# Four tap-row transfers replaced by one ScalarE copy, with a new table of priorities, in a four-layer encoder on one core

## The chip, the cores and the metric

One Trainium2 chip, of which the program uses a single core. The metric is device time in microseconds (us): the median of the runs, 1069.27 us before the change. The core's engines are TensorE (PE in the profile; PEld is its weight load), VectorE (DVE), ScalarE (ACT) and GpSimd (POOL); SyncE (SP) sends transfers, and its queue is SPq. The granted clock is the share of its full rate at which TensorE is allowed to run.

## The reference

The kernel computes a stack of four residual layers over x of 1 x 512 x 1024 in float32: differential attention, a Conformer convolution module, latent attention (MLA), and differential attention again. Every layer has one input projection, which also emits a SiLU gate, and one output projection. The change is in the second layer:

```python
def _conformer_conv(h, w_in, b_in, conv_w, conv_b, ln_g, ln_b, w_out):
    proj = h @ w_in + b_in
    a, b, gate = jnp.split(proj, 3, axis=-1)
    u = a * jax.nn.sigmoid(b)
    u = lax.conv_general_dilated(
        u, conv_w[:, None, :].astype(u.dtype), window_strides=(1,),
        padding=[(B_CONV - 1, 0)], dimension_numbers=('NWC', 'WIO', 'NWC'),
        feature_group_count=B_WIDTH) + conv_b
    u = jax.nn.silu(_layer_norm(u, ln_g, ln_b))
    return (u * jax.nn.silu(gate)) @ w_out
```

The convolution is depthwise: each of the 1024 channels has 31 taps of its own along the 512 positions. `b_conv_w` holds the taps, 31 rows by 1024 channels.

## The kernel before

Every fp32 product is made of three TensorE matmuls: both operands are split into a rounded high part and a low part, and hi·hi, lo·hi and hi·lo are added. In the profile these are the pairs on `Hh` and the single ones on `Hl`; such three matmuls of 512 columns are called a group below. A weight is loaded by SyncE (`..._w_r`), cast to its high part on ScalarE, and its low part is made by a subtraction on VectorE or GpSimd. The layers are named L0 to L3 in the program; the profile leaves the number away, so `L_qk_a` is the query and key projection's accumulator of some layer.

**The start of L0.** x is transposed on TensorE, 128 positions by four channel blocks at a time (`L0_tr00` to `L0_tr34`: the first digit is the block of positions, the second the first channel block). ScalarE copies a transpose into X and squares X, channel block by channel block in ascending order (`L0_sqs`, then `L0_sq1` to `sq7`); GpSimd adds the seven others to the first (line 521), and TensorE sums over the channels with `L0_ss`. The first square needs the blocks 0 to 3 of all positions, so nothing of this sum begins before `tr00`, `tr10`, `tr20` and `tr30` are done.

**The end of L0.** The last heads' attention, the gate's last chunk (`L0_g1`) and the first half of the output projection (`L0_o0`) are mixed. `L_ytr` transposes the gated heads, ScalarE makes the high part `L_y` of them (line 494), VectorE the low part (line 530), and `L_o` multiplies them with the output weights. The moves of `L_qk_st` (line 568) shift queries and keys between partitions for the last heads. In this place the tables of the second layer are prepared too: `L_rows` (taps and biases of `b_conv_w`, `b_conv_b`, `b_b_in`) is loaded and transposed to `L_vtr`.

**The convolution of L1.** Its eight channel blocks of 128 are handled by three engines, by the string 'DPDPDYYY': blocks 0, 2 and 4 on VectorE (a multiply and add per tap), blocks 1 and 3 on ScalarE and GpSimd (`L_ct`, `L_cq`), blocks 5, 6 and 7 on TensorE (`conv_phase`). For TensorE the input u is laid out in shifted phases by 48 moves on SyncE (`L_u<-L_u`, line 568; 16 for each block), and four taps at a time are multiplied as 32 x 32 diagonal matrices. The taps for those matrices come from `wx`, which `phase_weights` fills: `rows4` holds, for each of 12 sets of 32 channels, the 31 taps four times side by side; twelve TensorE transposes (`L_wxt`) turn it, and four ScalarE copies shift it into `wx`. `rows4` was loaded by four transfers from `b_conv_w` (line 562), each 31 x 12 x 32 elements, 46.5 KB in runs of 128 bytes. The profile shows both tiles, `L1_rows` and `L1_rows4`, as `L_rows`.

**What sets the order.** The program is written as a list of nodes in a `Plan` (class at line 362): each node has an engine, an assumed cost, and what it reads and writes. `Plan.order` (line 577) puts them into a fixed order on each engine. At each step it takes, among the engines' nodes whose inputs are done, the one that can begin earliest on its engine by the assumed costs; between nodes that can begin at the same time the smaller priority decides. A node's priority is its place in the program plus a number from the table `SHIFT` (lines 210 to 351), which has one entry for each tile and engine. Buffers come from rings with a fixed number of slots, so a load waits until a slot of its ring is free:

```python
key = (max(est2, f + 0.02), n.prio)
"raw": (3, [P, 2, 512], F32, True),
"big": (2, [P, 2048], F32, True),
```

The assumed cost of sending any transfer is 0.45 us. On the chip each engine works through its fixed order: an instruction that must wait holds back all that stands behind it.

## Time and profile before

| what | value |
|---|---|
| median of the runs | 1069.27 us (1068.98 to 1069.32, 3 runs) |
| the profiled execution | 1069.08 us |
| its span, first to last instruction | 1066.9 us |
| TensorE busy | 1009.4 us, 95% |
| VectorE, ScalarE, GpSimd busy | 771.9, 585.9, 209.4 us |
| mean granted clock | 0.984 |
| transfers | 87.72 MB in 75800 packets |

The profile is of one execution; 2.2 us of its time lie outside the span. A row of the waits names the engine, the tile for which it waited, and the one that released it, then the total, the number of times and the longest. A row of the timeline has start, duration, engine, line, operation, output<-inputs with their shapes, the count of instructions merged into it, and in brackets the idle time before it. A row of the windows has the stretch, its length, the busy time of PE, PEld, DVE, ACT and POOL with the number of instructions, the granted clock, the share of the transfer engines that was busy, and GB/s. A duration of a SyncE row is the time in its queue, not the landing.

### The profile page before, as it was taken

To read this page: it belongs to the slowest core of one execution; us is meant where nothing else is said; L and a number is where in the kernel's file an instruction comes from. 1 tells how busy PE (TensorE), PEld (TensorE's weight loads), DVE (VectorE), ACT (ScalarE), POOL (GpSimd) and SP (SyncE) were. 2 spreads that over 40 slices of the span, in tenths; PEclk is the share of its full clock that TensorE was granted. 3 is DMA by queue.
4 is the path that set the end of the run, shared out by engine and by line. 5 is a ranking of instruction groups with operands and counts; after the bars stand their busy time and mean duration, and the time that the engine had idled before them with its cause. 6 is when DMAs were issued, how large, how long until landed. Compare 5 with 4: busy or idle time off the path is not lost.

```text
span 1066.9 us, 15194 instructions
## 1 busy us (share of the span) xinstructions
PE 1009.4 (95%) x5212; PEld 848.7 (80%) x5212; DVE 771.9 (72%) x1966; ACT 585.9 (55%) x1225; POOL 209.4 (20%) x142
## 2 busy tenths in 40 slices
PE   8899999995999998897999999999999999999798
PEld 6788788874887877687888788878878888888687
DVE  4857699793758999958444659975574699989750
ACT  6457366655636555663434667745433755765742
POOL 2400000000004788972251000000210000000000
PEclk9899999997999999998999999999999999999999
DMA  8242242323014423311132221112332514232211
GB/s 242 80 137 61 79 117 62 102 73 96 31 30 131 108 83 95 102 40 60 33 116 65 74 60 41 41 38 80 96 103 79 148 43 126 80 100 76 63 40 60
DMA packets 75800, 87.72 MB, mean 82 GB/s; under 512 B 18601, under 2 KB 49193, under 8 KB 75724
## 3 DMA queue, kind: packets, MB, share of 16 engines
q1 hardware_dynamic: 75724, 86.76, 27.7%
q8 instruction: 41, 0.67, 0.3%
q14 instruction: 35, 0.29, 0.1%
HBM read 75.47 MB, written 2.10 MB: 73 GB/s over the span
## 4 chain that ended last, share of the span: by engine, by line
PE 65%; DVE 16%; ACT 6%; POOL 6%; issue 4%; DMA 2%; SPq 1%; DVEq 0%; ACTq 0%; POOLq 0%
PE L_o L464 19%; PE L_qk_a L464 14%; PE L_g_a L464 11%; PE L_v_a L464 7%; DVE L_c L530 5%; POOL L_cq L521 2%; POOL L_sqs L521 2%; SPq L562 1%; PE L_c_a L464 1%; PE L_qk_tr L470 1%; ACT G L494 1%; DVE L_u L530 1%; DVE L_g_w L518 1%; POOL L_o_w L521 1%; DMA L_setup<-a_lam_k 1%
## 5 line engine op out<-in xcount | busy, mean ns | idle before, releaser
L464 PE MATMUL L_qk_a<-L_qk_w,Hh 128*128 128x512 f32 x512 | 162.7, 398 | 3.5 <-DVE L_qk_T L518 1.3
L464 PE MATMUL L_o<-L_y,L_o_w 128*128 128x512 f32 x576 | 142.0, 397 | 0.0
L464 PEld LDWEIGHTS L_o<-L_y,L_o_w 128*128 128x128 f32 x576 | 106.5, 190 | 21.1 <-POOL L_o_w L521 0.4
L464 PE MATMUL L_g_a<-L_g_w,Hh 128*128 128x512 f32 x384 | 120.7, 395 | 1.1 <-ACT G L494 0.8
L744 POOL TENSOR_TENSOR L_h_or_y<-L_h_ov,minus_half 128x4 f32<-128x4 f32 x16 | 16.8, 1048 | 476.0 <-DVE L_h_ov L539 215.8
L464 PEld LDWEIGHTS L_qk_a<-L_qk_w,Hh 128*128 128x128 f32 x512 | 92.0, 188 | 21.5 <-DVE L_qk_T L518 1.5
L464 PE MATMUL L_qk_a<-L_qk_w,Hl 128*128 128x512 f32 x256 | 100.2, 392 | 0.2 <-DVE Hl L530 0.2
L521 POOL TENSOR_TENSOR L_cq<-L_cq,L_ct 128x512 f32<-128x512 f32 x58 | 83.6, 1442 | 23.6 <-ACT L_cq L494 16.4
L464 PE MATMUL L_v_a<-L_v_w,Hh 128*128 128x512 f32 x256 | 82.7, 405 | 0.0
L464 PEld LDWEIGHTS L_g_a<-L_g_w,Hh 128*128 128x128 f32 x384 | 70.2, 188 | 15.2 <-ACT G L494 1.2
L464 PE MATMUL L_ab_a<-Hh,L_ab_w 128*128 128x512 f32 x256 | 80.7, 391 | 1.6 <-DVE L_u L518 1.6
L464 PE MATMUL L_g_a<-L_g_w,Hl 128*128 128x512 f32 x192 | 75.0, 391 | 0.0
L521 POOL TENSOR_TENSOR L_sqs<-L_sqs,L_sq 128x512 f32<-128x512 f32 x28 | 44.7, 1597 | 122.2 <-ACT L_sq L494 68.9
L530 DVE SCALAR_TENSOR_TENSOR L_c<-L_u,L_tab,L_c 128x512 f32<-128x512 f32 x90 | 65.8, 750 | 1.4
L518 DVE TENSOR_TENSOR L_g_w<-L_g_w_r,L_g_w 128x1024 fp32r<-128x1024 f32 x32 | 42.8, 1339 | 33.0 <-ACT L_g_w L501 32.9
L494 ACT ACTIVATE L_ct<-L_u,L_tab 128x512 f32<-128x512 f32 x60 | 42.8, 723 | 34.9 <-POOL L_cq L521 33.0
L501 ACT CAST L_g_w<-L_g_w_r 128x1024 fp32r<-128x1024 f32 x32 | 33.7, 1054 | 46.2 <-PE L_v_a L464 28.3
L464 PEld LDWEIGHTS L_ab_a<-Hh,L_ab_w 128*128 128x128 f32 x256 | 48.1, 188 | 12.7 <-DVE L_u L518 1.7
L464 PEld LDWEIGHTS L_qk_a<-L_qk_w,Hl 128*128 128x128 f32 x256 | 48.1, 188 | 11.1 <-DVE Hl L530 0.7
L464 PEld LDWEIGHTS L_v_a<-L_v_w,Hh 128*128 128x128 f32 x256 | 47.8, 194 | 9.4 <-DVE L_qk_t L518 0.4
L501 ACT CAST L_o_w<-L_o_w_r 128x1024 fp32r<-128x1024 f32 x32 | 33.5, 1054 | 36.1 <-PE L_g_a L464 23.4
L464 PE MATMUL L_v_a<-L_v_w,Hl 128*128 128x512 f32 x128 | 50.9, 398 | 0.0
(366 smaller groups left out, 2339.7 us busy)
## 6 DMA issues: line engine op xcount, KB each, us to landing
L_qk_w_r<-a_w_in SPq DMA_DIRECT2D x62, 256.0 KB, 2.9
L_v_w_r<-a_w_in SPq DMA_DIRECT2D x16, 512.0 KB, 3.8
L_g_w_r<-a_w_in SPq DMA_DIRECT2D x16, 512.0 KB, 3.9
L_qk_st<-L_qk_st SPq DMA_DIRECT2D x32, 256.0 KB, 4.2
L_o_w_r<-a_w_out SPq DMA_DIRECT2D x16, 512.0 KB, 3.6
...
```

Of the source, the lines that this page charges most:

```text
L464: lambda nc: nc.tensor.matmul(out.real(), a.real(), b.real(), start=start, stop=stop),
L470: emit = lambda nc: nc.tensor.transpose(out.real(), src.real(), ident.real())
L494: nc.scalar.activation(out.real(), src.real(), func, scale=scale.real() if isinstance(scale, View) else scale, **kw)
L501: lambda nc: nc.scalar.copy(out.real(), src.real()), [src], [out])
L518: lambda nc: nc.vector.tensor_tensor(out=out.real(), in0=a.real(), in1=b.real(), op=op), [a, b], [out])
L521: lambda nc: nc.gpsimd.tensor_tensor(out=out.real(), in0=a.real(), in1=b.real(), op=op), [a, b], [out])
L530: self.add("dve", out.n / 960.0 + (0.13 if isinstance(scalar, View) else 0.068), lambda nc: nc.vector.scalar_tensor_tensor(out=out.real(), ...
L562: lambda nc: q(nc).dma_start(out.real(), src), [], [out],
L744: self.p.add("pool", 0.32 + 0.18 * v.n, lambda nc: nc.gpsimd.tensor_tensor(out=y.real(), in0=v.real(), in1=self.minus_half[:, 0:v.n].real( ...
```

## The change

`phase_weights` no longer loads `rows4`. One ScalarE copy reads the taps from `rows`, which holds them already, and writes each set of 32 channels four times. The inner variable of the last loop gets another name, since `rows` is now read there. All else in the program's text is the same but for the table `SHIFT`, of which every entry was searched anew; the lines behind it are one further down.

```diff
 SHIFT = {k: int(v) for k, v in (x.split("=") for x in """
-L0_g0_a.act=-1736 L0_g0_a.pe=28817 L0_g0_w.act=-2000 L0_g0_w.dve=13473 L0_g0_w_r.sp=323 L0_g1_a.act=19 L0_g1_a.pe=-69
+L0_g0_a.act=-797 L0_g0_a.pe=27679 L0_g0_w.act=699 L0_g0_w.dve=421 L0_g0_w_r.sp=4 L0_g1_a.act=686 L0_g1_a.pe=-1737
...
             rows4 = self.buf("big", L + "_rows4")
             n = 32 * 4 * len(ny)
             r4 = rows4[0:TAPS, 0:4 * n].split(1, 4 * len(ny)).split(2, NT)
-            src = d["b_conv_w"][0][:, P * ny[0]:P * ny[0] + n].rearrange("k (g c) -> k g c", c=32)
-            with p.only_when(after=self.mark):
-                for i in range(NT):
-                    p.load(r4[:, :, i, :], src, parts=TAPS)
+            p.copy(r4, rows[0:TAPS, P * ny[0]:P * ny[0] + n].split(1, 4 * len(ny)).over(2, NT))
...
             for i in range(NT):
-                rows = slice(32 * i, 32 * i + 32)
-                p.copy(self.wx[rows, :, 5 - i:5 - i + TAPS], tr[rows, :, 0:TAPS])
+                part = slice(32 * i, 32 * i + 32)
+                p.copy(self.wx[part, :, 5 - i:5 - i + TAPS], tr[part, :, 0:TAPS])
```

On SyncE, at the end of L0, the four transfers stood between the two moves of the first of the last pair of `L_qk_st` tiles (2423 and 2436 are buffer numbers). Before:

```order
L562 DMA L_rows<-b_conv_w 31x1024
L562 DMA L_rows<-b_conv_b 1x1024
L562 DMA L_o_w_r<-a_w_out 128x2x512
L562 DMA L_rows<-b_b_in 3x1024
L562 DMA L_o_w_r<-a_w_out 128x2x512
L568 DMA L_qk_st_2423<-L_qk_st_2423 64x2x512
L562 DMA L_rows_2476<-b_conv_w 31x12x32 x4
L568 DMA L_qk_st_2423<-L_qk_st_2423 64x2x512
L562 DMA L_o_w_r<-a_w_out 128x2x512
L568 DMA L_qk_st_2436<-L_qk_st_2436 64x2x512 x2
```

Now, on the same engine at the same place:

```order
L563 DMA L_rows<-b_conv_w 31x1024
L563 DMA L_rows<-b_conv_b 1x1024
L563 DMA L_rows<-b_b_in 3x1024
L563 DMA L_o_w_r<-a_w_out 128x2x512 x3
L569 DMA L_qk_st_2384<-L_qk_st_2384 64x2x512 x2
L569 DMA L_qk_st_2390<-L_qk_st_2390 64x2x512 x2
```

The transfers are gone and the moves follow one another behind three loads of output weights.

On ScalarE, in the same place of the changed kernel, the copy stands behind the casts of `L_qk_st`, and the order goes on with what feeds `L_o`:

```order
L502 CAST L_qk_st_2390<-L_qk_tr_2456 64x512 x2
L502 COPY L_rows_2484<-L_rows 31x1536
L495 ACTIVATE G<-L_g_a_2285,L_lay 128x512
L495 ACTIVATE G<-L_g_a_2319,L_lay 128x512
L502 CAST L_o_w_2508<-L_o_w_r 128x1024
L495 ACTIVATE G<-L_g_a_2327,L_lay 128x512
L495 ACTIVATE L_y_2511<-L_ytr_2512,L_lay 128x512
L502 CAST L_o_w_2539<-L_o_w_r 128x1024
L502 COPY wx<-L_wxt 32x12x31 x4
L495 ACTIVATE G<-L_g_a_2368,L_lay 128x512
L495 ACTIVATE L_y_2519<-L_ytr_2518,L_lay 128x512
L495 ACT_TABLE_LOAD
```

Before, both first `L_y` stood ahead of the `wx` copies, with no cast between them; now the second `L_y` stands behind them.

On TensorE, at the start of L0, the sum `L0_ss` has moved within the value projection (`L0_v0_a0` to `a3` are its four accumulators, `w0` and `w2` its weight tiles). Before:

```order
L464 MATMUL L0_v0_a1_479<-L0_v0_w0_416,Hh_115 128x512 x2
L464 MATMUL L0_v0_a1_479<-L0_v0_w0_416,Hl_116 128x512
L464 MATMUL L0_ss_499<-ones_110,L0_sqs_389 128x1 x4
L464 MATMUL L0_v0_a0_474<-L0_v0_w2_428,Hh_115 128x512 x2
L464 MATMUL L0_v0_a0_474<-L0_v0_w2_428,Hl_116 128x512
```

Now, where the third and fourth accumulators have had their first weights:

```order
L465 MATMUL L0_v0_a3_534<-L0_v0_w0_427,Hh_115 128x512 x2
L465 MATMUL L0_v0_a3_534<-L0_v0_w0_427,Hl_116 128x512
L465 MATMUL L0_ss_546<-ones_110,L0_sqs_425 128x1 x4
L465 MATMUL L0_v0_a2_529<-L0_v0_w2_440,Hh_115 128x512 x2
L465 MATMUL L0_v0_a2_529<-L0_v0_w2_440,Hl_116 128x512
```

47 groups of 512 columns now stand ahead of `L0_ss`, where there were 36. `L0_tr30`, the last transpose that its sum needs, has 24 groups ahead of it, where it had 12.

More of the change, by code (lines that the diff above doesn't have):

```diff
@@ L350 @@
[L350 to L351 removed]
+L0_g0_a.act=-797 L0_g0_a.pe=27679 L0_g0_w.act=699 L0_g0_w.dve=421 L0_g0_w_r.sp=4 L0_g1_a.act=686 L0_g1_a.pe=-1737
+L0_g1_w.act=-17687 L0_g1_w.dve=5407 L0_g1_w_r.sp=1853 L0_h0_cf.dve=1115 L0_h0_mx.dve=18445 L0_h0_or_y.dve=285
+L0_h0_or_y.pool=-148 L0_h0_osq.act=-1255 L0_h0_oss.dve=1970 L0_h0_ov.dve=-2061 L0_h0_p.act=-19371 L0_h0_p.dve=715
@@ new lines @@
+L0_sq1.act=-853 L0_sq2.act=-1682 L0_sq3.act=51 L0_sq4.act=-1492 L0_sq5.act=-6841 L0_sq6.act=-12265 L0_sq7.act=-113
+L0_sqs.act=-4123 L0_sqs.pool=855 L0_ss.pe=498 L0_tab.dve=1605 L0_tr00.act=-2249 L0_tr00.dve=-261 L0_tr00.pe=-660
+L0_tr04.act=7628 L0_tr04.dve=397 L0_tr04.pe=-464 L0_tr10.dve=1247 L0_tr10.pe=1621 L0_tr14.act=-2 L0_tr14.dve=16
+L0_tr14.pe=-1567 L0_tr20.act=2054 L0_tr20.dve=14311 L0_tr20.pe=-211 L0_tr24.act=-82 L0_tr24.dve=-1478 L0_tr24.pe=2469
+L0_tr30.act=1546 L0_tr30.dve=-697 L0_tr30.pe=6666 L0_tr34.dve=1430 L0_tr34.pe=-6766 L0_v.dve=-357 L0_v0_a.act=2173
@@ new lines @@
+L0_v0_a.pe=4196 L0_v0_w.act=-8640 L0_v0_w.dve=17753 L0_v0_w_r.sp=1940 L0_v1_a.pe=-11 L0_v1_w.act=-2629
+L0_v1_w.dve=-4317 L0_v1_w_r.sp=-1464 L0_warm.pe=-2323 L0_x0.sp=905 L0_x1.sp=3710 L0_y0.act=-5371 L0_y0.dve=-550
+L0_y1.act=5402 L0_y1.dve=-1346 L0_y2.act=-626 L0_y2.dve=-168 L0_y3.act=45 L0_y3.dve=-8438 L0_ytr0.pe=-58
+L0_ytr1.pe=43324 L0_ytr2.pe=-87 L0_ytr3.pe=2677 L0_ytr4.pe=-117 L0_ytr5.pe=-3428 L0_ytr6.pe=558 L0_ytr7.pe=3337
+L1_Rdg.dve=1438 L1_Rtr.pe=4873 L1_ab0_a.pe=-828 L1_ab0_sg.act=-2646 L1_ab0_sg.dve=-9 L1_ab0_w.act=3974
@@ new lines @@
+L1_yv5.act=-80 L1_yv5.dve=-5046 L1_yv6.act=3 L1_yv6.dve=11 L1_yv7.act=-221 L1_yv7.dve=1700 L2_c00_sq.act=5154
+L2_c00_t.dve=-1750 L2_c00_v.dve=354 L2_c00_y.pool=-2302 L2_c01_sq.act=2566 L2_c01_t.dve=200 L2_c01_v.dve=-454
+L2_c01_y.dve=141 L2_c01_y.pool=-152 L2_c02_sq.act=869 L2_c02_t.dve=1213 L2_c02_v.dve=201 L2_c02_y.dve=-2200
+L2_c02_y.pool=-995 L2_c03_sq.act=235 L2_c03_t.dve=-342 L2_c03_v.dve=1 L2_c03_y.dve=2310 L2_c0_a.pe=12049
+L2_c0_w.act=4119 L2_c0_w.dve=1733 L2_c0_w_r.sp=118 L2_g0_a.act=-202 L2_g0_a.pe=-1838 L2_g0_w.act=12338
@@ new lines @@
+L2_h4_sc.dve=3019 L2_h4_sc.pe=1703 L2_h4_wt.act=92 L2_h4_wtr.pe=-4947 L2_h5_mx.dve=2631 L2_h5_p.act=400
+L2_h5_sc.dve=9032 L2_h5_sc.pe=749 L2_h5_wt.act=-102 L2_h5_wtr.pe=3105 L2_h6_mx.dve=1605 L2_h6_p.act=-16
+L2_h6_sc.dve=-177 L2_h6_sc.pe=-2300 L2_h6_wt.act=1 L2_h6_wtr.pe=2339 L2_h7_mx.dve=-2036 L2_h7_p.act=-4509
+L2_h7_sc.dve=3784 L2_h7_sc.pe=-553 L2_h7_wt.act=4994 L2_h7_wtr.pe=-407 L2_kv0_T.act=22412 L2_kv0_T.dve=-163
+L2_kv0_a.act=67165 L2_kv0_a.pe=-1795 L2_kv0_sq.act=-2592 L2_kv0_ss.dve=-18030 L2_kv0_v.dve=-247 L2_kv0_w.act=946
@@ new lines @@
+L2_o1_w_r.sp=-1219 L2_o2.pe=-34 L2_o3.dve=3 L2_o3.pe=15177 L2_o4.dve=582 L2_o4.pe=455 L2_o5.dve=-7063 L2_o5.pe=809
+L2_o6.dve=-5715 L2_o7.dve=-2982 L2_o7.pe=-3122 L2_p0_rt.act=-24697 L2_p0_rt.dve=8862 L2_p0_st.act=-1591
+L2_p0_st.dve=-39 L2_p0_tr.pe=-415 L2_p1_rt.dve=-9767 L2_p1_rtr.pe=387 L2_p1_st.act=-1400 L2_p1_st.dve=-5005
+L2_p1_tr.pe=7 L2_p2_rt.act=-22836 L2_p2_rt.dve=-646 L2_p2_rtr.pe=-1382 L2_p2_st.act=-102 L2_p2_st.dve=-7210
+L2_p2_tr.pe=1394 L2_p3_rt.act=158 L2_p3_rt.dve=664 L2_p3_rtr.pe=-250 L2_p3_st.act=-1 L2_p3_st.dve=7860
@@ new lines @@
+L2_p3_tr.pe=-7090 L2_q0_T.act=-1005 L2_q0_T.dve=-17325 L2_q0_sq.act=-943 L2_q0_ss.dve=929 L2_q0_t.dve=-805
+L2_q0_v.dve=901 L2_q0_w.dve=10932 L2_q0_w_r.sp=1318 L2_q0_y.dve=180 L2_q1_T.act=1496 L2_q1_a.pe=2213 L2_q1_sq.act=1228
+L2_q1_ss.dve=43612 L2_q1_t.dve=95915 L2_q1_v.dve=-1642 L2_q1_w.act=1745 L2_q1_w.dve=-35 L2_q1_w_r.sp=2103
+L2_q1_y.dve=-8162 L2_q2_T.act=5 L2_q2_T.dve=28216 L2_q2_a.pe=10592 L2_q2_ss.dve=1894 L2_q2_t.dve=-5539
+L2_q2_v.dve=18338 L2_q2_w.act=-122 L2_q2_w.dve=503 L2_q2_w_r.sp=-7 L2_q2_y.dve=-50 L2_q3_T.act=-11988
@@ L352 @@
+L3_v0_a.act=-165 L3_v0_a.pe=-4 L3_v0_w.act=-3638 L3_v0_w.dve=-66 L3_v0_w_r.sp=-7 L3_v1_a.act=3056 L3_v1_a.pe=9277
+L3_v1_w.act=2427 L3_v1_w.dve=-13 L3_v1_w_r.sp=7813 L3_y0.act=-1042 L3_y1.act=4284 L3_y1.dve=-50 L3_y2.act=-30
+L3_y2.dve=-1702 L3_y3.dve=-20 L3_ytr0.pe=244 L3_ytr1.pe=-8 L3_ytr2.pe=5413 L3_ytr3.pe=1767 L3_ytr5.pe=-3471
+L3_ytr6.pe=234 L3_ytr7.pe=-11 none.act=578 none.dve=18020 none.sp=-2444
 """.split())}
```

245 lines of the change are left out of this document (105 added, 140 removed).

## The prediction

> **What bounds the kernel now.** I read the page first, for the share of each engine; then the waits of TensorE, to see where the rest of its time goes; then the chain and the timeline around the largest wait; then the granted clock in steps of 1 us.
>
> ```profile
> span 1066.9 us, 15194 instructions
> PE 1009.4 (95%) x5212; PEld 848.7 (80%) x5212; DVE 771.9 (72%) x1966; ACT 585.9 (55%) x1225; POOL 209.4 (20%) x142
> PEclk9899999997999999998999999999999999999999
> ```
>
> TensorE is busy for 1009.4 of 1066.9 us: it bounds the kernel, and the change adds and removes no matmul. So only two things can move the time: its 57.5 us of idle time, and the stretches in which its clock is low. The clock row has a 7 in its tenth slice (240 to 267 us). The waits of TensorE are (total, times, longest):
>
> ```profile
> PE L_wxt L470 <- DMA L_rows<-b_conv_w: 11.2, 1, 11.2
> PE L_ytr L470 <- DVE V L539: 4.7, 1, 4.7
> PE L_o L464 <- DVE V L530: 4.1, 2, 3.9
> PE L_ss L464 <- POOL L_sqs L521: 3.9, 3, 2.8
> PE L_g_a L464 <- ACT L_ct L494: 2.5, 1, 2.5
> ```
>
> One wait is a fifth of the idle time, and it is on exactly what the change removes: the twelve transposes L_wxt wait for the four transfers from b_conv_w. The chain of waits there (start, us, what) shows what the time is made of:
>
> ```profile
> 237.93 0.40 SPq L562
> 238.38 4.03 SPq L562
> 242.45 3.49 SPq L562
> 245.98 8.47 DMA L_rows<-b_conv_w
> ```
>
> SyncE's queue takes 3.5 to 4 us for each of these transfers, one behind the other, and the last one lands 8.47 us after its issue. Nothing ahead of them is late; they are themselves the work. The timeline of the same place, with TensorE, VectorE and ScalarE around it:
>
> ```profile
> 242.53 1.03 PE L470 MATMUL L_ytr<-ident,V 128*128 128x128 f32 x8
> 243.73 1.26 ACT L494 ACTIVATE L_y<-L_ytr,L_lay 128x512 fp32r<-128x512 f32 x2
> 245.11 1.41 DVE L530 SCALAR_TENSOR_TENSOR L_y<-L_ytr,L_lay,L_y 128x512 fp32r<-128x512 f32 x2
> 254.80 1.45 PE L470 MATMUL L_wxt<-ident,L_rows 31*128 31x31 f32 x12 [11.23 <-DMA L_rows<-b_conv_w]
> 256.29 1.91 ACT L501 COPY wx<-L_wxt 32x372 f32<-32x372 f32 x4 [10.72 <-PE L_wxt L470]
> 258.22 1.28 ACT L494 ACT_TABLE_LOAD   x1
> 259.51 1.91 ACT L494 ACTIVATE G<-G 128x2048 f32<-128x2048 f32 x1
> ```
>
> TensorE has nothing from 243.56 to 254.80, and VectorE and ScalarE run dry too (the last y is ready at 246.52). The stall costs more than its length, as the clock shows (window, us, busy time of PE, PEld, DVE, ACT, POOL, granted clock, DMA share, GB/s):
>
> ```profile
> 247.00:248.00 1.00, 0.00 (x0) 0.00 (x0) 0.00 (x0) 0.00 (x0) 0.00 (x0) 1.00 0.09 14
> 248.00:249.00 1.00, 0.00 (x0) 0.00 (x0) 0.00 (x0) 0.00 (x0) 0.00 (x0) 0.60 0.09 14
> 255.00:256.00 1.00, 1.00 (x12) 1.00 (x11) 0.00 (x0) 0.00 (x0) 0.00 (x0) 0.50 0.93 258
> 261.00:262.00 1.00, 1.00 (x4) 0.81 (x3) 0.55 (x3) 0.97 (x2) 0.00 (x0) 0.58 0.75 277
> 262.00:263.00 1.00, 1.00 (x6) 0.80 (x6) 1.00 (x4) 0.71 (x2) 0.00 (x0) 1.00 0.02 6
> ```
>
> The clock is full until 248.2, half from there to about 261.8, then full. TensorE works at half rate from 254.80 to 261.8: 7.0 us that hold 3.5 us of full-rate work, so 3.5 us are lost beside the 11.23.
>
> **The change, part by part.** *The four transfers go.* From the profiled execution's 1069.08 us (its span 1066.9 and 2.2 around it; the median of the runs is 1069.27, 0.2 more) that takes 11.23, and 3.5 for the clock if no long wait takes its place. The 11.4 us of issue on SyncE go as well; what stood behind them there (the moves of L_qk_st, the loads for L_o) is needed later and was waited for by nobody in the list above, so I count nothing for it.
>
> *One ScalarE copy comes.* It writes 31 x 1536 elements. No row has that size. The first row here is from the list of the tile L_rows (xcount, shortest/median/longest ns, first and last start), the others are the nearest in size (busy, mean ns):
>
> ```profile
> L562 SPq DMA_DIRECT2D L_rows<-b_conv_w x5: 362/3422/4030, 212.2 to 246.0; - x5
> L494 ACT ACTIVATE G<-G 128x2048 f32<-128x2048 f32 x6 | 11.5, 1914 | 0.1
> L501 ACT CAST L_g_w<-L_g_w_r 128x1024 fp32r<-128x1024 f32 x32 | 33.7, 1054 | 46.2 <-PE L_v_a L464 28.3
> ```
>
> Between 1.05 us (1024 elements) and 1.91 (2048), 1.48 by a straight line; the bounds are 1.05 and 1.91, since fewer partitions change nothing in either direction that these rows show. Its source is the first of the five transfers, sent at 212.2, 30 us ahead; so its place in ScalarE's queue decides. The order puts it directly behind the casts of L_qk_st, ahead of the gate's activations. On TensorE eight groups of L_g_a, a group being three matmuls, stand between the transposes for those casts and the first L_ytr; a group takes 0.68 us by the start's row below. That is 5.4 us, in which ScalarE has some casts, about 2.5 us, and the copy. So the copy ends about 2 us ahead of the first L_wxt, and its cost on TensorE's path is 0. Without that cover it would be at most its own 1.9 us.
>
> *What is late next.* With the stall gone, TensorE meets a chain on ScalarE that the stall had hidden. L_ytr ends at 243.56; the L_y half in ScalarE takes 0.63 (half of 1.26) and its low part 0.70 on VectorE, so that L_o can begin at about 245.1 (start 243.73 + 0.63 + 0.70). TensorE is through L_wxt at 244.3 (243.56 + half of 1.45): 0.8 us idle. Behind this ScalarE has in a row: a weight cast (1.05), the four copies into wx (1.91), one gate activation and one L_y (0.7 and 0.63), the table load (1.28), the 2048-wide activation (1.91) and the next L_y (0.63). From 245.0 these end at 253.1, and with the low part the third L_y is there at 253.8. TensorE has until then four groups of L_o (0.68 each) and 23 transposes (L_vtr, L_ytr, L_h5j_wtr; 1.03 for eight), 5.7 us from 245.1: it waits another 3.0. That makes 3.8; I take +3.0, since the cast in that row can come earlier, with bounds of 0 (ScalarE well ahead) and +6 (the row 2 us later).
>
> *The start is reordered.* Here the table of numbers, not the copy, moves something that the profile prices:
>
> ```profile
> 21.14 0.60 PE L470 MATMUL L_tr<-ident,L_x 128*128 128x128 f32 x4
> 20.46 0.62 PE L464 MATMUL L_qk_a<-L_qk_w,Hh 128*128 128x512 f32 x2
> 28.18 0.66 ACT L501 COPY X<-L_tr 128x512 f32<-128x512 f32 x1
> 33.14 9.88 POOL L521 TENSOR_TENSOR L_sqs<-L_sqs,L_sq 128x512 f32<-128x512 f32 x5 [0.18 <-ACT L_sq L494]
> 43.08 1.60 PE L464 MATMUL L_ss<-ones,L_sqs 128*128 128x1 f32 x8 [2.81 <-POOL L_sqs L521]
> 43.00:44.00 1.00, 0.92 (x6) 0.93 (x6) 0.94 (x3) 0.00 (x0) 0.02 (x1) 0.70 0.45 168
> 44.00:45.00 1.00, 1.00 (x5) 1.00 (x5) 1.00 (x3) 0.00 (x0) 0.00 (x0) 0.50 0.10 39
> 50.00:51.00 1.00, 1.00 (x6) 0.77 (x5) 0.85 (x5) 0.00 (x0) 0.00 (x0) 0.89 0.00 0
> ```
>
> A group takes 0.68 us (20.46 to 21.14). L_ss reaches its turn at 40.27 and waits 2.81 us for GpSimd's seven additions. After it the clock is half from 43.4 to 50.2, 6.8 us: 3.4 lost. In the new order 47 groups stand ahead of L_ss, not 36: 11 x 0.68 = 7.5 us later, at 47.8. But the last transpose that the sum needs, L0_tr30, stands behind 24 groups, not 12: 8.2 us later. Its copy X, 28.18 before, is not late by as much, since ScalarE reached it 7 us behind its transpose: about 32. Then seven additions of 1.3 to 2 us (9.88 for five), with weight casts in between, end at 46 to 48.5. So the wait shrinks from 2.81 to between 0 and 1; with it goes the half clock. Sum -2.3 to -6.2. Since VectorE's and ScalarE's order there is new too, I take -5.0, with bounds of -6.2 and +1.5.
>
> By the Trainium skill, "TensorE: Matmul & The Clock Gate", section "What's actually happening", the clock falls after an idle window of about 3.4 us. The rows have it fall behind 2.81 us of idle time, so the trace does not agree, unless the half clock here is not the wait's; by that rule the start would gain 2.3 and the sum would be 1055.1.
>
> *The rest of the table.* The remaining large waits (4.7 at L_ytr, 3.9 at L_o) have the same producers and neighbours in both orders, and the 1009 us of matmul are the same. In the convolution the moves of L_u stand closer together. I count 0, with bounds of -5 and +5, the size of the largest wait left.
>
> The sum: 1069.08 - 11.23 - 3.5 + 3.0 - 5.0 = 1052.4; I say 1052.5.
>
> **The rivals.** *The start keeps its wait* (L0_tr30 is later by as much as L_ss, and GpSimd's sum with it): 1069.08 - 11.73 = 1057.4, with 11.73 = 11.23 + 3.5 - 3.0. For it speaks that both moved by about the same, against it ScalarE's slack of 7 us. *The half clock at the start is not the wait's* and stays: 1069.08 - 11.73 - 2.3 = 1055.1 (2.3 is the wait of 2.81 less a rest of 0.5). Against it is that the clock is full through the wait and falls 0.3 us behind its end. The Trainium skill's rule of the idle window, named above, is what this rival would follow from. *The next chain costs more*: ScalarE's row is in the way by 6 us, and such a wait halves the clock again: 1069.08 - 11.23 + 6.0 - 5.0 = 1058.9, and 1061 where the start gains 3 only. *More is won*: no bubbles, the full 6.2, and 3 from the other waits: 1069.08 - 11.23 - 3.5 - 6.2 - 3 = 1045.
>
> *Slower*, by one mechanism: the 48 moves of L_u on SyncE in the convolution.
>
> ```profile
> 450.25 0.52 SPq L562 DMA_DIRECT2D L_o_w_r<-b_w_out  x1
> 450.82 19.80 SPq L568 DMA_DIRECT2D L_u<-L_u  x30
> 463.67 8.20 PE L464 MATMUL L_c<-L_wa,L_u 128*128 128x128 f32 x72
> 474.42 4.67 POOL L521 TENSOR_TENSOR L_o_w<-L_o_w_r,L_o_w 128x1024 fp32r<-128x1024 f32 x2 [5.50 <-ACT L_o_w L501]
> ```
>
> A move takes 0.66 us (19.80 / 30). All of them now stand behind two loads of L_o_w_r, and 34 behind a third. If that third load waited for its buffer until GpSimd had made a low part (on the old trace's time 474.42, of which 5.5 are a wait for ScalarE's cast and two additions of 1.4 now come later: about 467), the 34 moves would end at 467 + 22.4 and land at about 491. TensorE's first L_c block, 463.67 there, now has the eight gate groups ahead of it that stood between the blocks: it begins 8 x 0.68 = 5.4 later, at 469.1, and its last quarter (8.20 x 3/4 behind) at 475.3. It would wait 15 us and lose 3.5 of clock: 1052.5 + 18.5 = 1071. It decides from some 17 us of lateness on. Against it: a third load behind two others needs the buffer of L_g_w_r, which is free far earlier, as at 450.25. *The change doesn't do what it says*: the copy is released late, say 5 us behind its place, and L_wxt waits 3: 1055.5 with the same sum; a full return of the stall has no source.
>
> **How the numbers follow.** Forecast 0.50 (1049 to 1055); the start as before 0.18; the clock not the wait's 0.05; the next chain dearer 0.09; more won 0.13; the copy late 0.02; slower 0.03. The range 1043 to 1061 leaves out the ends of "more won", of "the next chain" and the slower case, under 2 in 10. This kernel's runs can tell 0.2%, 2.1 us, from no change: faster means under 1067.1. All cases but one lie there; for unseen mishaps I leave a little: faster 0.94, same 0.02, slower 0.04.
>
> **What would show it.** Right: no wait of L_wxt on a DMA, the copy of L_rows ended before the last L_g_a group; clock 1.00 through the end of the first layer; then waits of L_o of 0.5 to 3 us on L_y; L_ss near 48 us with under 1 us of wait and no half clock behind it. Wrong: L_wxt waits for ScalarE; the half clock is there again at either place; or a new wait above 5 us at the first L_c on L_u.

## The result and the profile after

The changed kernel takes 1062.95 us (median of 6 runs, 1059.47 to 1066.13), the kernel before 1069.12 us beside it (6 runs): a ratio of 0.9942, with a 95% interval of 0.9918 to 0.9965. It is faster by 6.2 us. The forecast was 16.6 us, and 1062.95 lies above the upper end of the range, 1061.

The page of the changed kernel, its head, TensorE's row and the row of the granted clock:

```profile
span 1062.4 us, 15183 instructions
PE 1010.8 (95%) x5212; PEld 847.7 (80%) x5212; DVE 764.4 (72%) x1966; ACT 586.1 (55%) x1226; POOL 216.0 (20%) x142
PEclk9999999998999999999999999999999999999899
```

The profiled execution took 1064.24 us. TensorE's work is the same, the 7 of the clock row has become an 8, and there is a new 8 near the end. The waits of TensorE (total, times, longest):

```profile
PE L_o L465 <- DVE V L531: 6.6, 2, 3.6
PE L_ytr L471 <- DVE V L540: 4.7, 1, 4.7
PE L_g_a L465 <- DVE G L519: 4.4, 3, 3.0
...
PE L_v_a L465 <- DVE L_qk_T L519: 2.1, 1, 2.1
...
PE L_c L465 <- DVE L_wa L519: 1.9, 1, 1.9
...
PE L_ss L465 <- POOL L_sqs L522: 1.7, 3, 1.0
```

The wait of 11.2 us of L_wxt has gone, and the one of 2.8 us of L_ss has shrunk. In their place stand a second long wait of L_o on V (6.6 in two, where there were 4.1 in two of 3.9 and 0.2), one of L_v_a on L_qk_T, and one of L_c on its weights L_wa. The timeline of the changed kernel at the end of layer 0, where the transfers had stalled it:

```profile
237.91 1.48 ACT L502 COPY L_rows<-L_rows 31x1536 f32<-31x1536 f32 x1
...
242.20 0.94 PE L471 MATMUL L_wxt<-ident,L_rows 31*128 31x31 f32 x12
...
243.78 0.73 PE L465 MATMUL L_o<-L_y,L_o_w 128*128 128x512 f32 x2 [0.23 <-DVE L_y L531]
...
248.17 1.91 ACT L495 ACTIVATE G<-G 128x2048 f32<-128x2048 f32 x1
...
250.12 1.12 DVE L531 SCALAR_TENSOR_TENSOR V<-L_o,L_h_or_y,G 128x128 f32<-128x128 f32 x4 [2.47 <-ACT G L495]
...
251.29 1.65 PE L465 MATMUL L_o<-V,L_h5j_wt 128*128 128x128 f32 x6 [3.02 <-DVE V L531]
```

The copy takes 1.48 us and ends at 239.39, 2.81 ahead of the first L_wxt, which waits for nothing. ScalarE's row then ends in the 2048-wide activation of the gate; V needs it; and L_o of the next head needs the PSUM buffer that V reads. TensorE stands for 3.02 us. The windows of 1 us there (columns as before: length, busy PE, PEld, DVE, ACT, POOL, granted clock, DMA share, GB/s):

```profile
249.00:250.00 1.00, 0.00 (x0) 0.00 (x0) 0.00 (x0) 1.00 (x2) 0.00 (x0) 1.00 0.92 340
250.00:251.00 1.00, 0.00 (x0) 0.00 (x0) 0.88 (x4) 1.00 (x3) 0.00 (x0) 0.67 0.27 100
...
253.00:254.00 1.00, 1.00 (x6) 1.00 (x5) 0.00 (x0) 0.98 (x5) 0.00 (x0) 0.50 0.06 16
...
257.00:258.00 1.00, 1.00 (x10) 1.00 (x10) 0.89 (x5) 1.00 (x4) 0.00 (x0) 0.91 0.00 0
```

The clock is half again, from 250.3 to 257.2. So the place keeps 3.25 us of waits and 2.9 us of clock.

A ledger by stage makes the rest comparable. For each stretch of the program it adds TensorE's idle time and half of the time in which it was busy at half clock, both from the trace (the half clock ahead of the first rise and the time behind the last matmul are left out); the stretches are divided at equal amounts of matmul work and named by the time of the kernel before. Each column is one execution:

| stage (us of before) | before | changed | E1 | E9 | E12 |
|---|---|---|---|---|---|
| 0 to 60, start of L0 | 11.1 | 9.6 | 11.1 | 6.4 | 6.2 |
| 60 to 230, rest of L0 | 3.4 | 3.0 | 3.4 | 3.4 | 3.4 |
| 230 to 300, end of L0 | 14.9 | 6.2 | 3.1 | 5.1 | 2.0 |
| 300 to 425, L1 to the first gate groups | 5.6 | 3.4 | 4.1 | 4.1 | 4.1 |
| 425 to 520, convolution, end of L1 | 12.7 | 16.5 | 13.4 | 13.3 | 10.9 |
| 520 to 700, L2 | 8.6 | 10.1 | 6.9 | 7.0 | 6.9 |
| 700 to 970, end of L2, L3 | 2.1 | 0.9 | 1.8 | 1.7 | 0.9 |
| 970 on, end of L3 | 8.8 | 11.4 | 11.9 | 8.9 | 11.1 |

E1, E9 and E12 are experiments below. Against the kernel before, the changed one wins 8.7 at the end of L0 and 1.5 at the start, and gives back 3.8 in the convolution's stage, 1.5 in L2 and 2.6 at the end of L3; the useless matmuls of E12 count as work, not as loss. One or two windows of half clock (3.4 us each) that an execution happens to have move an entry by up to 1.7 or 3.4.

### The profile page after: what moved, and what is told of

Read it like the earlier page. It is cut to its first block, busy times and chain, and to the rows that moved or that the text cites. A ratio compares the mean times of both kernels' runs of the same rounds, so it can differ in the third digit from the quotient of the medians.

```text
span 1062.4 us, 15183 instructions
## 1 busy us (share of the span) xinstructions
PE 1010.8 (95%) x5212; PEld 847.7 (80%) x5212; DVE 764.4 (72%) x1966; ACT 586.1 (55%) x1226; POOL 216.0 (20%) x142
## 4 chain that ended last, share of the span: by engine, by line
PE 70%; POOL 8%; ACT 8%; DVE 5%; issue 4%; DMA 2%; SPq 2%; DVEq 0%; ACTq 0%; POOLq 0%
PE L_o L465 21%; PE L_qk_a L465 15%; PE L_g_a L465 10%; PE L_v_a L465 7%; PE L_ab_a L465 5%; POOL L_cq L522 4%; POOL L_sqs L522 2%; ACT G L495 1%; SPq L569 1%; PE L_c_a L465 1%; PE L_qk_tr L471 1%; PE L_h7j_sc L465 1%; PE L_h2j_sc L465 1%; PE L_h6j_sc L465 1%; DMA L_setup<-a_lam_k 1%
## 5 line engine op out<-in xcount | busy, mean ns | idle before, releaser
L519 DVE TENSOR_TENSOR L_g_w<-L_g_w_r,L_g_w 128x1024 fp32r<-128x1024 f32 x32 | 43.5, 1360 | 28.9 <-ACT L_g_w L502 28.8
L465 PEld LDWEIGHTS L_ab_a<-Hh,L_ab_w 128*128 128x128 f32 x256 | 48.1, 188 | 10.1
L502 ACT CAST L_qk_w<-L_qk_w_r 128x1024 fp32r<-128x1024 f32 (+1 forms) x33 | 33.7, 1037 | 36.3 <-PE L_o L465 14.6
```

What stands on the lines that cost most here:

```text
L465: lambda nc: nc.tensor.matmul(out.real(), a.real(), b.real(), start=start, stop=stop),
L502: lambda nc: nc.scalar.copy(out.real(), src.real()), [src], [out])
L519: lambda nc: nc.vector.tensor_tensor(out=out.real(), in0=a.real(), in1=b.real(), op=op), [a, b], [out])
```

## The experiments

The theory after the result: the copy does what the prediction says, and the new table of priorities, which the prediction had winning 5 us, loses several instead. The rival: the chain behind the copy, which any order would meet, is dearer than 3 us. All kernels below are the changed kernel with another order of its nodes on the engines, and all compute the whole result. For that the program builds both orders once: `after` is the list that the new table gives, `before` the one that the old table gives, with the copy put behind ScalarE's last cast of L_qk_st. `splice(a, b, n)` takes the first n nodes of a and then the others in the order of b, `of` picks nodes by name and engine, and `put` moves nodes on one engine behind a given one. E4, E8, E11 and E12 also do some of the work more than once. The diffs show only the lines that matter, against a program that gives the changed kernel's order.

**E1: the old order with the copy.**

```diff
-    plan.order(forced=[plan.nodes[s] for s in after])
+    plan.order(forced=[plan.nodes[s] for s in before])
```

> The order of every engine as before, with one difference: the four transfers are gone from SyncE and the one ScalarE copy stands behind the last cast of L_qk_st. Theory A (the copy alone removes the stall; what limits the gain is the row of work on ScalarE and the half clock that its wait brings; the new table gives little): the 11.2 us wait of L_wxt is 0, a wait of 1 to 3 us of L_o on ScalarE's gate takes its place, and the kernel takes 1057 to 1061 us, so about as much as or less than the changed kernel's 1062.95. Theory B (the copy needs the new order around it to be hidden): L_wxt waits for ScalarE, and the time is 1064 or more.

It took 1056.63 us (1056.40 to 1058.29; ratio 0.9895, 0.9883 to 0.9908): 6.3 us less than the changed kernel by the medians, 5.0 by the two ratios to the kernel before beside each, and 0.4 below theory A's range. The same lateness of ScalarE is there, but TensorE takes it in three pieces, and the clock stays full. First two rows of E1's timeline, then a window:

```profile
245.80 0.50 PE L465 MATMUL L_o<-L_y,L_o_w 128*128 128x512 f32 x1 [1.20 <-ACT L_y L495]
...
252.52 0.94 PE L465 MATMUL L_o<-V,L_h5j_wt 128*128 128x128 f32 x6 [1.39 <-DVE V L531]
```

```profile
253.00:254.00 1.00, 1.00 (x13) 1.00 (x11) 0.79 (x2) 0.50 (x4) 0.00 (x0) 1.00 0.00 0
```

The pieces are 1.20, 0.38 and 1.39, together 2.97, and no window there is at half clock. The copy alone is the larger gain, and the table costs 5 to 6 us on top of it.

**E2: the new order with the four transfers.**

```diff
-            p.copy(r4, rows[0:TAPS, P * ny[0]:P * ny[0] + n].split(1, 4 * len(ny)).over(2, NT))
+                for i in range(NT):
+                    p.load(r4[:, :, i, :], src, parts=TAPS)
```

> The changed kernel's order on every engine, but the copy taken out and the four transfers back on SyncE behind the first move of the last pair of L_qk_st, where they stood. Theory A: the stall is the transfers' own: L_wxt waits 12 to 14 us, the clock halves for two or more windows, and the kernel takes 1072 to 1077 us. Theory B (the new table would have hidden the transfers, too): a wait under 5 us, 1062 to 1067 us.

It took 1079.56 us (1077.65 to 1083.16; ratio 1.0111, 1.0094 to 1.0127), the only kernel here that is slower than before, and 2.6 above theory A's range; the wait too is longer than the 12 to 14 us expected. A row of its waits, and one of its timeline:

```profile
PE L_wxt L471 <- DMA L_rows<-b_conv_w: 16.5, 1, 16.5
```

```profile
239.05 14.01 SPq L563 DMA_DIRECT2D L_rows<-b_conv_w  x4
```

Two things make the wait longer by 5.3 us. TensorE runs dry 2.8 us behind the start of the transfers (at 241.89), in the kernel before 5.6 behind it (237.93 to 243.56); and the four hold SyncE's queue for 14.01 us, before for 11.47. The copy is worth 11.7 us in the old order (1068.3, the kernel before beside E1, to 1056.6) and 16.6 in the new one (1079.6 to 1063.0).

**E3: the gate's activation earlier on ScalarE**, in the changed kernel: the last gate chunk, the table load and the 2048-wide activation are put ahead of a weight cast and the four copies into wx; what reads them on VectorE moves along.

```diff
+    first = [of("L0_g1_a3", "act")[0], of("L0_y1", "act")[0], of("L0_y0", "dve")[0], of("L0_y1", "dve")[0], silu]
+    first += of("L0_o0_w6", "act") + of("L0_o0_w6", "dve")
+    seq[i:i] = first
```

> The changed kernel with another order on ScalarE in one place: the fourth gate activation, the second L_y and the 2048-wide activation (with its table load) stand ahead of the weight cast and of the four copies into wx. Theory A (the 3.0 us wait of L_o for V at the end of the first layer is ScalarE's queue, and the half clock behind it is that wait's): the 2048-wide activation begins at about 245 instead of 248.2, L_o waits for V under 1 us, perhaps 1 us later for an L_y, the half clock behind it (6.8 us, 2.9 lost) is gone, and the kernel takes 1057 to 1060 us. Theory B (V is late for another reason, VectorE or the single buffer of L_o): the wait stays near 3 us and the time at 1061 to 1065.

It took 1062.03 us (1060.59 to 1067.58; ratio 0.9953, 0.9935 to 0.9972), which can't be told from the changed kernel. The activation begins at 245.21, not 248.17. But a low part on VectorE, moved with the cast it needs, waited for that cast in front of two others:

```profile
248.09 1.22 DVE L519 TENSOR_TENSOR L_o_w<-L_o_w_r,L_o_w 128x1024 fp32r<-128x1024 f32 x1 [3.41 <-ACT L_o_w L502]
249.23 0.44 DVE L505 COPY L_tab<-L_vtr 128x280 f32<-128x280 f32 x1
...
249.73 0.83 PE L471 MATMUL L_ytr<-ident,V 128*128 128x128 f32 x4 [2.00 <-DVE L_tab L505]
...
250.77 1.65 PE L465 MATMUL L_o<-V,L_h5j_wt 128*128 128x128 f32 x6 [0.21 <-DVE V L531]
```

The wait on V went down to 0.21, and one of 2.00 on the copy L_tab came in its place. So the wait for V does follow ScalarE's queue, as theory A has it, but the edit did not test what that wait costs. E8 asks it in another way.

**E4: the copy written twice**, in the changed kernel.

```diff
+    copy.emit = copy.emit * 2
```

> The changed kernel with the new ScalarE copy written twice, one behind the other: 1.48 us more work on ScalarE at that place. Theory A (ScalarE is the engine that ends last there, so the copy is not free): the wait of L_o for V grows from 3.0 to 4.2 to 4.6 us and the kernel takes 1 to 3 us longer, 1064 to 1066. Theory B (as the prediction had it: the copy is hidden under eight groups of TensorE work): the wait stays at 3.0 and the time at 1063.

It took 1063.98 us (1061.28 to 1066.39; ratio 0.9956, 0.9941 to 0.9971), again not to be told from the changed kernel. But the trace shows that the second copy is not hidden. A row of E4's timeline:

```profile
247.46 0.50 PE L465 MATMUL L_o<-L_y,L_o_w 128*128 128x512 f32 x1 [1.18 <-ACT L_y L495]
```

The first L_y ends 3.03 us behind the start of L_ytr (244.37 to 247.40), in the changed kernel 1.63 behind it (241.23 to 242.86), and the first L_o waits 1.18 for it, where it did not wait. L_wxt still waits for nothing, so the cover ahead of it holds. The wait for V does not grow as theory A had it: it is 0.37, since TensorE now comes later to it, held up by that wait and by half clock from 249.1 to 255.9. The copy stands in ScalarE's row ahead of L_y, and what is added there does reach TensorE.

**E5 and E6: the new order up to a point, then the old one.** E5 takes the new order for the start of L0, to about 60 us; E6 for all of layer 0 and the beginning of layer 1, to about 290 us.

```diff
-    plan.order(forced=[plan.nodes[s] for s in after])
+    plan.order(forced=[plan.nodes[s] for s in splice(after, before, 284)])      # E5
+    plan.order(forced=[plan.nodes[s] for s in splice(after, before, 1507)])     # E6
```

> One copy and the old order (1056.6 us), but the first 60 us or so in the changed kernel's order: the start as the new table has it, the rest as before. Theory A (the losses of TensorE, idle time and half clock together, add up place by place; in the profiles the start lost 11.1 us in the old order and 9.6 in the new): 1.5 us less, 1054 to 1056. Theory B (the start is worth the 5 us of the prediction, and the new order gives them back later): 1051 to 1053.

> The changed kernel's order to about 290 us, the end of the first layer; behind that the old order. Theory A (the new table also costs time in the later layers: by the profiles 3.1 us more is lost at the end of the convolution, 3.0 more in the third layer, 2.1 less elsewhere): about 4 us less than the changed kernel, 1058 to 1060. Theory B (what the new table costs lies at the end of the first layer alone): 1062 to 1064, as the changed kernel.

E5 took 1055.55 us (1054.68 to 1061.9; 0.9876, 0.9861 to 0.9890), E6 1059.48 us (1055.8 to 1066.32; 0.9915, 0.9889 to 0.9941). By the medians the new start is worth 1.1 us against E1 (not resolved, their intervals overlap), the rest of the first layer costs 3.9, and the later layers cost 3.5 more (to 1062.95). That the start isn't where the 6.3 us go is shown; the split between the other two is not sharp, since E6's interval overlaps those of its neighbours. Its runs spread over 10 us, and its profiled execution, 1055.8, shows a likely reason. First a row of its timeline, then a window:

```profile
250.62 0.94 PE L465 MATMUL L_o<-V,L_h5j_wt 128*128 128x128 f32 x6 [2.99 <-DVE V L531]
```

```profile
251.00:252.00 1.00, 1.00 (x12) 1.00 (x11) 0.89 (x2) 0.40 (x3) 0.00 (x0) 1.00 0.21 78
```

It is the same wait of 3 us as in the changed kernel, and here the clock stays full behind it. A wait of this length halves the clock in one profile and not in the other.

**E7: the preparation out of the way**, from E1: the copy and L_wxt with its copies into wx are moved behind the end of L0.

```diff
+    put(q, "act", of("L1_rows4", "act"), of("L0_h7_osq", "act")[-1])
+    put(q, "pe", of("L1_wxt", "pe"), of("L0_o12", "pe")[0])
+    put(q, "act", of("L1_wxt", "act"), of("L1_sqs", "act")[0])
```

> One copy and the old order (1056.6 us), but the copy, the twelve transposes L_wxt and the four copies into wx stand later: at 287 to 300 us, where ScalarE is idle 4.2, 2.8 and 3.5 us at a time, and not at the end of the first layer's heads. Theory A (ScalarE is what ends last there, with 19 of 20 us busy; 3.4 us of it are this preparation): the waits of L_o for L_y (1.2 us) and for V (1.4 us) there shrink to under 0.5 each, nothing waits later, 1054 to 1055.5. Theory B (other work ends last there): 1056 to 1057.

It took 1055.99 us (1052.40 to 1058.31; 0.9883, 0.9866 to 0.9900), 0.6 less than E1, inside the spread: what the preparation costs there is at most 1 to 2 us, and it isn't resolved. In its profile the wait of L_ss, 2.61 us, halves the clock for one window of 3.4 us (43.5 to 46.9), not for two as in the kernel before.

**E8: the 3 us wait filled.** In the changed kernel the eight transposes L_ytr ahead of that wait are written four times; the extra work is of no use to the result, and ends before V is ready.

```diff
+        if n.eng == "pe" and n.label in ("L0_ytr1", "L0_ytr3"):
+            n.emit = n.emit * 4
```

> The changed kernel, with the eight L_ytr transposes ahead of the 3.0 us wait of L_o for V written four times each (the same result four times): TensorE is busy for 2.5 to 3 us of that wait. Theory A (the half clock from 250.3 to 257.1, which cost 2.9 us, comes of that idle time alone): the clock is full there, L_o begins at the same time as before, 1059.5 to 1061. Theory B (the clock falls for another reason, or the second pair of L_y, late by the longer transposes, takes the gain): 1063 to 1065.

It took 1060.47 us (1058.89 to 1064.66; 0.9927, 0.9913 to 0.9942), 2.5 below the changed kernel by the medians, though their intervals overlap. Its timeline, then its window:

```profile
247.00 3.65 PE L471 MATMUL L_ytr<-ident,V 128*128 128x128 f32 x32
...
251.05 0.94 PE L465 MATMUL L_o<-V,L_h5j_wt 128*128 128x128 f32 x6 [0.40 <-DVE V L531]
```

```profile
253.00:254.00 1.00, 1.00 (x6) 0.87 (x7) 0.47 (x3) 0.50 (x2) 0.00 (x0) 1.00 0.00 0
```

L_o begins 251.05, 0.24 earlier than in the changed kernel, so the end of the wait is where it was. What goes is the half clock behind it, and by the start times of the same matmuls in the two profiles 2.3 us are won between 240 and 258 us. That the 24 useless transposes kept the clock up isn't shown by this one profile: without them the clock's grid (last section) would have divided the wait here nearly as in E6, with TensorE busy for 0.62 and 0.50 of the two windows, and there the clock stayed full. In favour of it: with them the shares are 1.00 and 0.88, and over all six executions the mean granted clock is 0.990 (0.989 to 0.992), in the changed kernel 0.988 (0.986 to 0.990).

**E9: the sums later.** From E1, L_ss moves eight groups back on TensorE, behind groups of L_v_a whose weights and PSUM buffers are ready.

```diff
+    ss = next(n for n in pe if n.label == "L0_ss")
+    ahead = [n for n in pe if n.label in ("L0_v0_a0", "L0_v0_a1") and pe.index(n) > pe.index(ss)][:8]
+    put(q, "pe", ahead + [ss], pe[pe.index(ss) - 1])
```

> The order before on every engine, with the copy (the kernel that ran at 1056.6 us), and one move: the sum of squares' four matmuls, which stood 2.80 us behind L_sqs of GpSimd at 40.4 us and brought two windows of half clock, are put eight groups of L_v_a (24 matmuls, 5.4 us at full clock) later on TensorE, and these eight use only weights and PSUM buffers that are ready by 40.5 us. Theory A (the prediction's term of the start was right in kind: the wait and its half clock can be had, and it was the new table that did not get them): the 2.8 us are filled, at most 0.6 us of a wait on a PSUM buffer of L_qk_T is left behind it, and the clock stays full at 43 to 51 us: 1056.6 - 2.3 - (1.7 to 3.4) = 1051 to 1052.7 us. Theory B (the wait only covered a second one, as the changed kernel's wait of 2.14 us on L_qk_T suggests): VectorE gives the PSUM buffers back later because GpSimd and the sums are later, the wait appears at L_v_a with its half clock, and the time stays at 1055.5 to 1057.5 us.

It took 1053.51 us (1052.82 to 1055.28; 0.9862, 0.9848 to 0.9876), 3.1 below E1 and between the two theories' ranges. A row of its timeline, then a window:

```profile
48.35 0.70 PE L465 MATMUL L_v_a<-L_v_w,Hh 128*128 128x512 f32 x2 [1.54 <-DVE L_qk_T L519]
```

```profile
49.00:50.00 1.00, 1.00 (x6) 0.85 (x5) 1.00 (x3) 0.00 (x0) 0.00 (x0) 1.00 0.08 16
```

L_ss waits for nothing; 1.54 us (not the 0.6 expected) come back behind it as a wait on the PSUM buffer of L_qk_T, and the clock is full. E11 and E12, which have the same move, have full clock there too; the kernel before, E1 and E7, which do not, all have it halved. The stage's loss falls from 11.1 to 6.4, by 4.7, near the 5.0 that the prediction had put down to the new table. In the profiled execution 2.0 us of it are lost again at the end of L0. A row of its timeline and a window there:

```profile
241.19 0.50 PE L465 MATMUL L_o<-L_y,L_o_w 128*128 128x512 f32 x1 [1.16 <-ACT L_y L495]
```

```profile
243.00:244.00 1.00, 1.00 (x9) 0.88 (x8) 0.00 (x0) 0.97 (x2) 0.00 (x0) 0.50 1.02 387
```

The clock is half there from 242.2 to 249.0, behind the same two short waits (1.16 and 0.37) at which E1 kept full clock.

**E10: the set-up products later.** In the changed kernel VectorE makes L_tab for layer 2 in the middle of the convolution. The rows of the changed kernel's timeline:

```profile
466.40 3.24 DVE L519 TENSOR_TENSOR L_tab<-L_setup 128x256 f32<-128x256 f32 x2
469.56 1.34 DVE L519 TENSOR_TENSOR L_wa<-L_d,wx 128x1152 f32<-128x1152 f32 x1
...
470.96 11.28 PE L465 MATMUL L_c<-L_wa,L_u 128*128 128x128 f32 x84 [1.85 <-DVE L_wa L519]
```

```diff
+    tab = [n for n in q["dve"] if n.label == "L2_tab"]
+    put(q, "dve", tab, of("L1_wa7_3", "dve")[0])
```

> The changed kernel with one move on VectorE: the six products of L_tab for layer 2 (3.24 us in a row at 466.4 us, 4.3 us in all) are put behind the last L_wa of layer 1. Theory A (what the later layers lose by the new table is lost where such a move of set-up work delays the convolution's weights: 1.85 us of wait before L_c at 469.1 us and the window of half clock behind it, 1.7 us): the wait before L_c falls below 0.7 us, no window of half clock near 472 us, and the time is 1062.4 - 1.9 - 1.7 = about 1058.8 us (1058 to 1060.5, where the window comes in only some runs). Theory B (that wait only takes the place of the one at the end of layer 1, 4 to 5 us before L_ytr, which is as long as before): the convolution ends earlier, but V and its statistics end no earlier, the wait before L_ytr grows by as much, and the time stays at 1061.5 to 1063.5 us.

It took 1060.84 us (1059.99 to 1065.25; 0.9934, 0.9918 to 0.9949), 2.1 below the changed kernel by the medians (the intervals overlap) and just above theory A's range. Its timeline:

```profile
459.83 18.81 PE L465 MATMUL L_c<-L_wa,L_u 128*128 128x128 f32 x167
...
487.86 4.49 PE L471 MATMUL L_ytr<-ident,V 128*128 128x128 f32 x17 [4.67 <-DVE V L540]
```

The convolution runs through, the wait before L_ytr is as long as before (4.67), and the stage's loss falls from 16.5 to 13.1. Against the changed kernel's profile the same matmuls start 0.5 us earlier at 460 us and 4.3 earlier at 480 us, and 4.2 are left at 1040 us. So in these two executions the wait of L_c and the half clock behind it were lost time, and the table had made the wait.

**E11: useless work in two more waits.** From E7 with the move of E9: 30 transposes of the identity ahead of the first L_ytr of L1 (the 4.7 us wait), and L_ytr ahead of the 3.9 us wait in L3 written seven times.

```diff
+            n.emit = [lambda nc: nc.tensor.transpose(out.real[:, 0:P], one[:, :], one[:, :])] * 30 + n.emit
+        if n.eng == "pe" and n.label == "L3_ytr2":
+            n.emit = n.emit * 7
```

> The order before with the copy prepared later (1056.0 us, its profiled run 1052.4), the sum of squares eight groups later on TensorE, and matmuls that are of no use to the result written into the two longest waits that then have half clock behind them: 30 transposes of the identity ahead of the first L_ytr of layer 1 (a wait of 4.7 us) and six more times the L_ytr ahead of the 3.9 us wait at the end of layer 3. Theory A (half a window's idling is what halves the clock, so a wait that must stay costs only its own length if TensorE is kept busy in it): 1.7 us of half clock gone at the start with 2.3 us of wait, 3.4 us gone at 480 us, up to 3.4 us at 975 us: from the profiled run 1052.4 - 10.8 = 1041.6 us, from the median 1056.0 - 10 = 1046; 1041 to 1047 us. Theory B (the extra matmuls hold up what follows, or the windows move to the next waits): 1050 to 1056 us.

It took 1054.47 us (1050.89 to 1056.61; 0.9869, 0.9850 to 0.9889), 7.5 us above theory A's range and inside theory B's. At the end of L1 the clock is full at 480 to 490 us, but nothing ends earlier. The timeline of E11:

```profile
479.35 3.44 PE L1659 MATMUL L_ytr<-ident 128*128 128x128 f32 x30
...
484.11 3.90 PE L471 MATMUL L_ytr<-ident,V 128*128 128x128 f32 x20 [1.32 <-DVE V L540]
...
489.24 0.66 PE L471 MATMUL L_ytr<-ident,V 128*128 128x128 f32 x4 [1.23 <-ACT L_yv L495]
...
492.38 7.93 PE L465 MATMUL L_o<-L_y,L_o_w 128*128 128x512 f32 x31
```

The L_ytr transposes run at full rate and then wait longer for ScalarE to take their results (L_yv). L_o begins 13.0 us behind the convolution's end (479.35 to 492.38); in E7, at half clock, it was 12.5 (477.25 to 489.76). ScalarE sets the pace in this place, the half clock had cost nothing that shows, and so there was nothing to win. The second place did win: in L3 the wait shrinks from 3.88 to 1.26, the clock is full where E7 has it half from 975.3 to 982.2, and between 975 and 983 us TensorE gains 1.3 us on E7.

**E12: useless work where TensorE sets the pace.** From E9: nine transposes of the identity ahead of the first L_o at the end of L0, and the two L_ctr blocks at 425 us written three times.

```diff
+        if n.eng == "pe" and n.label in ("L1_ctr0", "L1_ctr1"):
+            n.emit = n.emit * 3
+    first.emit = [lambda nc: nc.tensor.transpose(out.real[:, 0:P], one[:, :], one[:, :])] * 9 + first.emit
```

> The order before with the copy and the sums later (1053.5 us, its profiled run 1052.8), with matmuls of no use to the result in two waits whose half clock falls on matmuls that no other engine paces: nine transposes of the identity ahead of the first L_o at the end of layer 0 (a wait of 1.16 us at 240 us, half clock from 242.2 to 249.0 with TensorE busy throughout) and the two L_ctr blocks at 425.4 us written three times (a wait of 2.46 us, half clock from 429.9 to 433.4). Where they were put before (end of layers 1 and 3) the clock stayed full in two of three windows but ScalarE's and VectorE's work on the results set the pace, and the end did not move. Theory A (half clock costs its 1.7 us for each window only where TensorE itself sets the pace; there a filled wait gives it back): both stretches at full clock, 3.4 + 1.7 us less in the profiled run, some of it lost again as the wait for V at the end of layer 0 (up to 2 us): 1048 to 1051.5 us. Theory B (the half windows move to the next waits, or the stretches were paced by the other engines as well): 1052.5 to 1055 us.

It took 1051.98 us (1049.62 to 1053.11; 0.9841, 0.9824 to 0.9857), the fastest here: by the medians 16.5 us below the kernel before beside it, 11.0 below the changed one and 1.5 below E9, between the two theories' ranges. The timeline of E12 at the two places:

```profile
239.65 1.20 PE L1657 MATMUL L_o<-ident 128*128 128x128 f32 x9
...
247.65 0.94 PE L465 MATMUL L_o<-V,L_h5j_wt 128*128 128x128 f32 x6 [1.41 <-DVE V L531]
...
427.31 0.47 PE L465 MATMUL L_g_a<-Hh,L_g_w 128*128 128x512 f32 x1 [0.75 <-ACT L_ct L495]
...
434.71 0.51 PE L465 MATMUL L_g_a<-Hh,L_g_w 128*128 128x512 f32 x1 [1.65 <-DVE G L519]
```

Both stretches run at full clock; 1.41 us come back as the wait on V, as expected, and 1.65 at the second place as a wait on G. The two stages lose 3.1 and 2.4 less than in E9, but part of that is the useless work itself, in the place of idle time. By the start times of the same matmuls in the two profiles 1.3 us are won at the first place and 0.7 at the second. But the end of L3 loses 2.2 more (11.1 against 8.9): the clock is half there from 971.2 to 978.0 and from 984.8 to 988.3, in E9 from 976.1 to 979.5 only. Theory A is right in kind at the two places, but for less than its 3.4 and 1.7 us, and theory B's "next waits" take back most of it.

## Why the prediction was wrong

**The copy's terms were right.** -11.23 for the wait, -3.5 for the clock behind it and +3.0 for the next chain give 1057.35 from 1069.08; E1, which has these alone, took 1056.63, and the ledger of its stage fell by 11.8 (14.9 to 3.1), where 11.7 were forecast. The copy's 1.48 us and its place ahead of L_wxt (2.8 us to spare, about 2 predicted) are as worked out. The chain was 2.97 us in E1 and 3.25 in the changed kernel. Its cause was only half named: the last and longest piece is not L_o waiting for L_y, but L_o waiting for the PSUM buffer that V reads, and V for the 2048-wide activation; that the size came out is in part luck. Luck too is the full clock behind it in E1: E5 and E9, with the same order there, have windows of half clock.

**The step that failed is the table's: "The start is reordered", -5.0, and "The rest of the table", 0.** Together they were +6.3 by the medians (1056.63 to 1062.95), 11 us away from the estimate.

*The start* won 1.5 us in the profile's ledger and 1.1 by E5's median, and neither is resolved: over all profiles the ledger of this stage is 7.8 to 13.0 in the eight that start in the new order and 8.0 to 11.1 in the three with the old one. L_ss was to reach its turn at 47.8; it did so at 50.07, since 2.14 us of a wait of L_v_a now stand ahead of it. GpSimd was to end at 46 to 48.5; it ended at 50.98. The rows of the changed kernel's timeline:

```profile
35.66 3.63 POOL L522 TENSOR_TENSOR L_sqs<-L_sqs,L_sq 128x512 f32<-128x512 f32 x1 [11.90 <-ACT L_sq L495]
...
41.97 9.01 POOL L522 TENSOR_TENSOR L_sqs<-L_sqs,L_sq 128x512 f32<-128x512 f32 x5 [0.65 <-ACT L_sq L495]
...
47.01 0.72 PE L465 MATMUL L_v_a<-L_v_w,Hh 128*128 128x512 f32 x2 [2.14 <-DVE L_qk_T L519]
...
51.03 1.05 PE L465 MATMUL L_ss<-ones,L_sqs 128*128 128x1 f32 x8 [0.96 <-POOL L_sqs L522]
```

The first addition began at 35.66, 2.8 us behind the copy X (32.87, where the estimate had about 32), and took 3.63 us, where 1.3 to 2 were assumed; why it took so long isn't settled (two subtractions of VectorE for L_v_w run beside it). I had moved L_ss along TensorE's queue and asked only whether its own producer is ready, not whether the groups now ahead of it have their PSUM buffers. The two waits together, 3.1 us, are longer than the 2.81 they replace; the clock is half for one window (52.4 to 55.8) and not for two. E9 shows that the wait and its half clock were there to be won, by a move on TensorE alone: 4.7 us in its profile and 3.1 by the medians, and the new table was not what gets it.

*The rest*, counted as 0 with bounds of 5, cost +7.4 by the medians (E5's 1055.55 to 1062.95), beyond the bound. Against E1 three places lose about 3 each: the end of L0 (6.2 against 3.1), the convolution (16.5 against 13.4) and L2 (10.1 against 6.9). Whether that is the order or one execution's clock, the same ledger over the other profiles tells. The convolution's stage loses 15.3 to 16.6 in the five profiles that have the new order there unchanged, and 12.7 to 14.5 in the six with the old one; L2 loses 9.3 to 10.2 in six and 6.9 to 8.6 in eight. These two are the order's. For the convolution E10 shows a cause in the profile, set-up products ahead of its weights on VectorE. "Same producers and neighbours" was said of TensorE's waits; it didn't hold for VectorE's queue, which I had not followed there. For L2 no run tests a cause.

The end of L0 is not shown to be dearer in the new order. Its 3.1 is half clock: E6, with the new order there, loses 3.2, and E5 and E9, with the old one, 3.3 and 5.1. Behind the single wait of 3.0 us the clock fell in two of three profiles (changed, E10; not E6), behind two shorter waits of 1.2 to 1.5 and 0.4 in four of six (E4, E5, E9, E11; not E1, E7). So the pieces of E1 are no remedy by themselves.

**The rivals.** "The next chain costs more" came true in its second half: it asked for a wait of 6 us and a halved clock, and a wait of 3 us was enough for that in the profiled execution. "The start keeps its wait", given 0.18, is nearer to what happened than the forecast, but its time of 1057.4 has no loss for the rest. The slower rival did not occur: the first L_c waits for nothing on L_u. The Trainium skill's rule on the clock ("TensorE: Matmul & The Clock Gate", "What's actually happening"), by which the half clock at the start would not have been the wait's, does not hold here: with the wait gone in E9 the clock stays full.
